# A top-1 attention kernel on one core: half-width screening while the keys load, and a rearranged tail

## Chip, cores, metric

One core of a Trainium2 chip (trn2). The metric is device time in microseconds (us) of one execution, taken from the chip. Engines are called as in the profile: PE (TensorE), PEld (its weight loads), ACT (ScalarE), DVE (VectorE), POOL (GpSimd), SP (SyncE). "Fold" below means the VectorE instruction that writes `W` for one tile of 128 query rows; there are 128 tiles (4 batches of 32), so the starts of the folds are 128 clock marks spread over the run, and nearly every reading below uses them.

## The reference

```python
def setup_inputs():
    B, Sq, Sk, D = 4, 4096, 4096, 128      # q, k, v: randn, float32, fixed seed

def reference(q, k, v):
    logits = np.matmul(q, k.transpose(0, 2, 1))
    best = np.argmax(logits, axis=-1)
    b_idx = np.arange(q.shape[0])[:, None]
    return v[b_idx, best, :].astype(np.float32)
```

For each query row: the key with the largest dot product, and that key's row of `v`.

## The kernel before

The kernel screens groups of four keys in fp16 (the product of a query tile with sums and differences of keys, absolute values, a maximum of 8 per row), then gathers the candidate group, works out its exact dots on VectorE, and gathers the row of `v`. Rows whose best two groups are too near ("flagged") are computed again in fp32 at the end of each half. The parts that the change touches, with cuts:

```python
LATE = 5
...
    def put_first(b, h):                      # first key of each group, negated, for the differences
        ...
        nc.vector.tensor_scalar(out=kd[:, h, :, 0, :], in0=src[:, :, 0, :], scalar1=-1.0, scalar2=None, op0=OP.mult)
...
    def dpart(t, x):                          # differences: product and absolute value
        if t >= T:
            return
        ps = pp.tile([P, 1024], FP32, tag="u", name=f"pd_{t}_{x}")
        mm(ps, t, 1 + 2 * x, True)
        A = ep.tile([P, 1024], FP16, tag=f"A{x}", name=f"A_{t}_{x}")
        nc.scalar.activation(out=A, in_=ps, func=AF.Abs)
        A_t[t, x] = A

    def spart(t, x):                          # sums, plus A; x == 0 leaves PSUM through ScalarE as E
        ...
    def fold(t):                              # x == 1 is folded with E into W on VectorE
        E, ps = E_t.pop(t)
        nc.vector.scalar_tensor_tensor(out=W_t[t % NW].bitcast(I16)[:, 1::2], in0=ps, scalar=QSCALE, in1=E,
                                       op0=OP.mult, op1=OP.max)

    def top(t):
        nc.vector.max(out=TOP[:, t, :], in_=W_t[t % NW].bitcast(FP32))
...
    def dots(c, x, m):                        # exact dots of m tiles at once: prod, p, p, D
        ...
    def flags_last(t0, t1, ready, fill, late):   # flagged rows of the second half, at the very end
        ...
        OH = fp.tile([P, SLOTS, P], FP16, tag="OHe", name="OH_e")
        for z in range(SLOTS):
            nc.vector.tensor_scalar(out=OH[:, z], in0=iota_h, scalar1=posn[:, z:z + 1], scalar2=None, op0=OP.is_equal)
        ...                                   # TensorE adds up fq_e from OH
        fill()
        ...                                   # gb_e, rs_e, row_e read fq_e
        late(LATE)                            # so many waiting gathers of v rows go ahead of FK
        get(FK[:, 0, :], k_flat, gb[:, 0:1], B * Sk)
        get(FQ, q_flat, row, P * T)
        for r in (1, 2):
            get(FK[:, r, :], k_flat, gb[:, r:r + 1], B * Sk)
        yield
        ...                                   # dots of FK with FQ, index xw_fe
        get(FV, v_flat, win, B * Sk)
        nc.gpsimd.indirect_dma_start(out=out_flat, out_offset=IOA(ap=rowk, axis=0), in_=FV, in_offset=None, ...)
...
    put_k(0, 0)                               # head: second half of the first batch's keys
    for u in (1, 3, 0, 2):
        trn_half(u, 1, (0, 1))
    trn_half(1, 1, (2, 3), by_act)
    trn_half(3, 1, (2, 3), by_dve)
    trn_half(0, 1, (2, 3), by_dve)
    trn_half(2, 1, (2, 3), by_dve)
    dpart(0, 0)
    dpart(0, 1)
...
            m = 4 if t1 <= 108 else 2         # tiles per dots
...
    screen(T)                                 # tail
    top(T - 2)
    gathers(T - 2)
    flush()
    fold(T - 1)
    ...
    end = flags_last(T // 2, T, last_picks, lambda: dots_whole(0), late_now)
    next(end)
    dots_whole(1)
    pick_whole()
```

Of the kernel before, what the change touches and what calls it, by code (L numbers as in the profile page):

```python
# [7 lines left out]
FP32 = mybir.dt.float32  # L8
FP16 = mybir.dt.float16
# [6 lines left out]
OP = mybir.AluOpType  # L16
AF = mybir.ActivationFunctionType
# [4 lines left out]
TAU = 8.0  # L22
NEAR = 0.5
SLOTS = 6
LATE = 5
NKG = 6


# [1 line left out]
def kernel(ctx, tc, q, k, v, out):  # L30
    nc = tc.nc
    B, Sq, D = q.shape
    Sk = k.shape[1]
    P = 128
    NQT = Sq // P
    T = B * NQT
# [10 lines left out]
    pp = ctx.enter_context(tc.tile_pool(name="ps", bufs=4, space=bass.MemoryType.PSUM))  # L47
    ep = ctx.enter_context(tc.tile_pool(name="ev", bufs=3))
    rp = ctx.enter_context(tc.tile_pool(name="ref", bufs=2))
    sp = ctx.enter_context(tc.tile_pool(name="sml", bufs=4))  # L50
    fp = ctx.enter_context(tc.tile_pool(name="flag", bufs=1))
# [6 lines left out]
    kT = [bp.tile([P, Sk], FP16, name=f"kT{i}", tag=f"kT{i}") for i in range(2)]  # L58
    qT = [bp.tile([P, Sq], FP16, name=f"qT{i}", tag=f"qT{i}") for i in range(2)]
    natk = [bp.tile([P, 2, 16, P], FP16, name=f"natk{i}", tag=f"natk{i}") for i in range(2)]  # L60
    kd = bp.tile([P, 2, 4, 3, P], FP16, name="kd", tag="kd")
# [9 lines left out]
    def put_k(b, h):  # L71
        if b >= B:
            return
        src = natk[b % 2][:, h].rearrange("p (g f) d -> p g f d", f=4)
        nc.vector.tensor_tensor(out=kd[:, h], in0=src[:, :, 1:4, :], in1=src[:, :, 0:1, :].to_broadcast([P, 4, 3, P]),
                                op=OP.subtract)
        kb16 = k16[b].rearrange("(h p n) d -> p h (n d)", p=P, n=16)
        nc.sync.dma_start(out=kb16[:, h], in_=kd[:, h].rearrange("p g f d -> p (g f d)"))

    def put_first(b, h):  # L80
        if b >= B:
            return
        src = natk[b % 2][:, h].rearrange("p (g f) d -> p g f d", f=4)
        nc.vector.tensor_scalar(out=kd[:, h, :, 0, :], in0=src[:, :, 0, :], scalar1=-1.0, scalar2=None, op0=OP.mult)
        kb16 = k16[b].rearrange("(r x) d -> r (x d)", x=4).rearrange("(h p g) (f d) -> p h g f d", h=2, p=P, f=3)
        for f in range(3):
            nc.sync.dma_start(out=kb16[:, h, :, f, :], in_=kd[:, h, :, 0, :])
# [22 lines left out]
    for i in range(2):  # L110
        ps = pp.tile([P, 1024], FP32, tag="u", name=f"warm_{i}")
# [33 lines left out]
    iota_h = cp.tile([P, P], FP16, tag="iota_h")  # L145
# [5 lines left out]
    for h in range(2):  # L151
# [3 lines left out]
                            op0=OP.mult, op1=OP.add)  # L155
# [20 lines left out]
    def trn_half(u, h, ms, put=None):  # L176
        x = 2 * (u // 2)
        if ms[0] == 0:
            tk_t[u] = pp.tile([P, 512], FP32, tag="u", name=f"tk_{u}_{h}")
        ps = tk_t[u]  # L180
        for m in ms:
            o = ps[:, m * P:(m + 1) * P]
            nc.tensor.matmul(out=o, lhsT=natk[0][:, h, 4 * m + x, :], rhs=identh, start=True, stop=False)
            nc.tensor.matmul(out=o, lhsT=natk[0][:, h, 4 * m + x + 1, :],
                             rhs=identn if u % 2 else identh, start=False, stop=True)
        if put is not None:
            put(kT[0][:, u * 1024 + h * 512:u * 1024 + h * 512 + 512], ps)
# [31 lines left out]
    A_t = {}  # L219
    st = {}  # L220

    def mm(ps, t, u, stop):
        b, qt = t // NQT, t % NQT
        for n in range(2):
            nc.tensor.matmul(out=ps[:, n * 512:(n + 1) * 512], lhsT=qT[b % 2][:, qt * P:(qt + 1) * P],  # L225
                             rhs=kT[b % 2][:, u * 1024 + n * 512:u * 1024 + (n + 1) * 512], start=True, stop=stop)

    def dpart(t, x):
        if t >= T:
            return  # L230
        ps = pp.tile([P, 1024], FP32, tag="u", name=f"pd_{t}_{x}")
        mm(ps, t, 1 + 2 * x, True)
# [3 lines that stand above are left out]
# [16 lines left out]
    def screen(t):  # L252
        dpart(t, 0)
        spart(t - 1, 0)
        dpart(t, 1)
        spart(t - 1, 1)
# [6 lines left out]
    def top(t):  # L263
        nc.vector.max(out=TOP[:, t, :], in_=W_t[t % NW].bitcast(FP32))  # L264
# [201 lines left out]
    def flags_last(t0, t1, ready, fill, late):  # L466
# [16 lines left out]
        ps = pp.tile([P, 1024], FP32, tag="u", name="fp_e")  # L483
        nc.tensor.matmul(out=ps[:, 0:1], lhsT=tri, rhs=n2[:, 0:1], start=True, stop=True)  # L484
        for r in range(1, 4):
# [5 lines left out]
                                op0=OP.is_ge, op1=OP.mult)  # L491
        posn = fp.tile([P, SLOTS], FP32, tag="posn", name="posn_e")
# [2 lines left out]
                                       scalar=-2.0 * Sk, in1=e8[:, 1:4, 0:SLOTS].rearrange("p r s -> p s r"),  # L495
                                       op0=OP.mult, op1=OP.add)
        OH = fp.tile([P, SLOTS, P], FP16, tag="OHe", name="OH_e")
        for z in range(SLOTS):
            nc.vector.tensor_scalar(out=OH[:, z], in0=iota_h, scalar1=posn[:, z:z + 1], scalar2=None, op0=OP.is_equal)
        ps2 = pp.tile([P, 1024], FP32, tag="u", name="fq_e")  # L500
        for s in range(SLOTS):
# [12 lines left out]

        late(LATE)
        get(FK[:, 0, :], k_flat, gb[:, 0:1], B * Sk)
# [49 lines left out]
    def dots_whole(i):  # L566
        for f in range(4):
            pr = fp.tile([P, P], FP32, tag="xp", name=f"xp_w_{i}_{f}", bufs=2)
            nc.vector.tensor_tensor_reduce(out=pr, in0=X_t[i][:, f * P:(f + 1) * P], in1=q32[:, i, :], scale=1.0, scalar=0.0,
                                           op0=OP.mult, op1=OP.add, accum_out=XD[:, i, f:f + 1])  # L570
# [94 lines left out]
    ALL = range(4)  # L665
# [2 lines left out]
    trn_half(0, 0, ALL, by_act)  # L668
    trn_q(0, 4, by_dve)
    trn_half(2, 0, ALL, by_act)  # L670
    put_k(0, 0)
    for u in (1, 3, 0, 2):
        trn_half(u, 1, (0, 1))
    trn_half(1, 1, (2, 3), by_act)
    trn_half(3, 1, (2, 3), by_dve)
    trn_half(0, 1, (2, 3), by_dve)
    trn_half(2, 1, (2, 3), by_dve)
    dpart(0, 0)
    dpart(0, 1)
    nc.vector.tensor_copy(out=iota_h, in_=iota_r)  # L680
    nc.vector.tensor_copy(out=rec2[:, :, 1], in_=iota_p.to_broadcast([P, SLOTS]))
    cuts = list(range(0, 96 + 1, 8)) + list(range(96 + 4, T - 3, 4)) + [T - 2, T]
    chunks = list(zip(cuts[:-1], cuts[1:]))
# [45 lines left out]
    def take_late(n):  # L729
        while n > 0 and late_q:  # L730
            g = late_q.pop(0)
            n -= g not in stores
            g()
        while late_q and late_q[0] in stores:
            wait_q.append((clock[0] + 2, late_q.pop(0)))
# [3 lines left out]
    def put_out(now):  # L739
        while wait_q and wait_q[0][0] <= now:  # L740
            wait_q.pop(0)[1]()

    def issue(it):
        n = 0
        clock[0] = it
        put_out(it)
        behind = len([g for g in near_q if g not in marks]) > (2 if it >= TAIL else 4)
        while near_q and (n < 1 + behind or near_q[0] in marks or it >= T - 1):
            g = near_q.pop(0)
            n += g not in marks  # L750
            g()
        if fast and it >= rest[0]:
            fast.pop(0)()
            rest[0] = it + 2
            n += 1
        if it < 16:
            take_late(2 if n == 0 and len(late_q) > 4 else 1)
            return
        b, qt = it // NQT, it % NQT
        busy = 0.7 if qt % 2 == 0 and (10 <= qt < 18 and b + 1 < B or 18 <= qt < 26 and b + 2 < B) else 0.0  # L760
        if qt in (13, 17) and b + 1 < B:
            busy += 1.0
        rate = 2.45 if it < 72 else 2.65 if it < 80 else 2.45 if it < 96 else 2.6 if it < 104 else 2.45 if it < 112 else 2.6
        room[0] = min(room[0] + rate - busy, 3.0) - n
        for i in range(2):
            if room[0] >= 1 and late_q and it < T - 1:
                take_late(1)
                room[0] -= 1
# [3 lines left out]
    def gathers(t):  # L772
        if t >= T - 2:
            gather_whole(t)
        for c, (t0, t1) in enumerate(chunks):
            m = 4 if t1 <= 108 else 2
            if t0 <= t < t1 and t < T - 2 and (t - t0) % m == m - 1:
                gather(c, t - m + 1, m)
            if t == t0 and t < T - 2:
                start(pick(c, t0, t1), "pick", c)  # L780
        if t % 8 == 7:
            put_rec(t - 7, t + 1)
        if t == SEGS[1] - 1:
            last = [c for c, x in enumerate(chunks) if x[1] == t + 1][0]
            start(flag_segment(0, t + 1, lambda: ("cnt", last) in done, lambda: ("out", last) in done), "flags")
# [3 lines left out]
    for b in range(1, B):  # L789
        x = b * NQT  # L790
        units += [(x - 1, x - NQT + (6 + 3 * i // 2 if b == 1 else 1 + 2 * i), unit_k, b, i) for i in range(16)]
    for it in range(T):
        b, qt = it // NQT, it % NQT
# [7 lines left out]
        if open_units:  # L801
            u = min(open_units)
# [35 lines left out]
    def late_now(n):  # L838
        take_late(n)
        put_out(1 << 20)  # L840

    def drain(group):
        for s in group:
            while True:
                try:
                    y = next(s["g"])
                except StopIteration:
                    live.remove(s)
                    break
                if y[0] == "until":  # L850
                    assert y[1]()

    def left(kind):
        return [s for s in live if s["kind"] == kind]

    screen(T)
    top(T - 2)
    gathers(T - 2)
    flush()
# [8 lines left out]
        drain(left("dots"))  # L868
        drain(left("pick"))

    end = flags_last(T // 2, T, last_picks, lambda: dots_whole(0), late_now)
    next(end)
    dots_whole(1)
    pick_whole()
    for _ in end:
# [32 lines left out]
```

## Time and profile before

| | before |
|---|---|
| median of the timed runs beside the kernel after | 440.71 us (440.14 to 441.29, 4 runs) |
| the profiled execution | 439.86 us, span 437.9 us, granted clock 0.964 |
| first fold; fold of tile 2; fold of tile 126 | 16.46; 21.96; 402.10 us |
| first candidate gather of tiles 122/123 on GpSimd | 399.17 us |
| first FK gather; FV gather; last scatter | 419.12; 429.59; 433.66 us |

A line of a timeline reads: start, duration, engine, line of the kernel, operation, output <- input, shapes, number of instructions merged into the line, and in brackets the idle time of that engine just before it and what ended it. A line of the groups by line has busy time and the mean of one instruction in ns. In the tail, kg, vr and xk are gathers of candidate groups, of values and of whole key rows; FK, FQ and FV are those of keys, queries and values for the flagged rows. The row list is the index `row_e` that the FQ gather reads; it is the last of the indices to come. A transfer lands when the profile shows its data as arrived.

### The profile page before, as it was taken

The numbers are of one execution on the slowest core, as the hardware profiler recorded it, in microseconds if no ns is written. First come the engines' busy times: TensorE is split into PE (matmuls) and PEld (weight loads), VectorE is DVE, ScalarE is ACT, GpSimd is POOL, SyncE is SP. The second block draws the span as 40 slices with busy tenths as digits, with TensorE's granted clock in tenths as the row PEclk, the third lists the DMA queues.
The fourth block names the chain that finished last, engine by engine and source line by source line (L and its number), as shares of the span: only waits on it lengthen the run. The fifth ranks groups of instructions, "written<-read, shape, count | busy, mean of one in ns | idle before, by whom it ended". The sixth has DMA issues, their size and how long they took to land.

```text
span 437.9 us, 6167 instructions
## 1 busy us (share of the span) xinstructions
PE 378.8 (87%) x1830; PEld 168.2 (38%) x1830; DVE 407.8 (93%) x734; ACT 375.5 (86%) x437; POOL 304.9 (70%) x335
## 2 busy tenths in 40 slices
PE   8999999999999999999999889989889888896010
PEld 4444444444444444444444334434333333332010
DVE  2688999999999999999999999999999999999971
ACT  2899999999999999999999789999998988896000
POOL 8513466677757886777777776777777777777773
PEclk9999999999999999999999999999999999999555
DMA  7943999463325999763326985362322332233341
GB/s 124 198 107 67 152 151 149 97 120 86 107 66 130 167 168 188 125 123 103 89 82 150 166 154 115 91 144 81 113 81 82 89 90 84 87 101 99 106 131 55
DMA packets 52868, 50.54 MB, mean 115 GB/s; under 512 B 34136, under 2 KB 40890, under 8 KB 52832
## 3 DMA queue, kind: packets, MB, share of 16 engines
q0 software_dynamic: 19072, 33.87, 38.5%
q1 hardware_dynamic: 33760, 16.26, 14.9%
q8 instruction: 14, 0.23, 0.2%
q14 instruction: 22, 0.18, 0.1%
HBM read 40.05 MB, written 14.55 MB: 125 GB/s over the span
## 4 chain that ended last, share of the span: by engine, by line
ACT 41%; issue 19%; DVE 16%; PE 14%; DMA 6%; POOL 3%; POOLq 0%; ACTq 0%; DVEq 0%; SPq 0%
ACT A L234 34%; ACT E L247 7%; DVE TOP L264 6%; PE psn L225 5%; PE psn L244 4%; DVE W L260 4%; PE pd L225 4%; DMA natk<-in_k_dram 2%; DMA FK<-in_k_dram,gb_e 2%; DMA out_dram<-vr 1%; DVE prod L300 1%; POOL vr L342 1%; POOL kg L282 1%; DVE p L305 1%; DVE D L310 1%
## 5 line engine op out<-in xcount | busy, mean ns | idle before, releaser
L234 ACT ACTIVATE A<-pd 128x1024 f16<-128x1024 f32 x256 | 260.2, 1045 | 13.7 <-PE pd L225 13.4
L282 POOL DMA_INDIRECT kg<-k,cand x126 | 125.5, 996 | 80.1 <-DVE cand L276 49.3
L260 DVE SCALAR_TENSOR_TENSOR W<-psn,E 128x1024 int16<-128x1024 f32 x128 | 166.2, 1298 | 7.2 <-ACT E L247 5.2
L225 PE MATMUL psn<-kT,qT 128*128 128x512 f16 x512 | 151.9, 378 | 13.8 <-ACT A L234 6.0
L225 PE MATMUL pd<-kT,qT 128*128 128x512 f16 x512 | 151.9, 378 | 8.9 <-ACT A L234 8.6
L225 PEld LDWEIGHTS <-qT 128*128 128x128 f16 x1024 | 97.9, 97 | 154.0 <-issue 64.0
L264 DVE MAX8 TOP<-W 128x8 f32<-128x1024 f32 x128 | 155.9, 1218 | 0.0
L342 POOL DMA_INDIRECT vr<-in_v_dram,win x126 | 125.2, 994 | 40.4 <-issue 33.5
L244 PE MATMUL psn<-A,identh 128*128 128x512 f16 x512 | 152.0, 378 | 0.0
L247 ACT ACTIVATE E<-psn 128x1024 int16<-128x1024 f32 x128 | 132.4, 1034 | 3.3 <-PE psn L244 3.0
L244 PEld LDWEIGHTS <-identh 128*128 128x128 f16 x512 | 49.6, 97 | 60.8
L300 DVE TENSOR_TENSOR prod<-kg,natq 128x768 f16<-128x768 f16 x63 | 34.4, 546 | 0.0
L205 ACT ACTIVATE kT<-uk 128x256 f16<-128x256 f32 x48 | 20.5, 427 | 1.5 <-PE uk L202 1.5
L305 DVE TENSOR_TENSOR p<-prod 128x768 f16<-128x768 f16 (+1 forms) x36 | 17.9, 497 | 0.1
L310 DVE TENSOR_REDUCE D<-p 128x12 f32<-128x384 f16 (+1 forms) x36 | 17.5, 486 | 0.1
L201 PE MATMUL uk<-identh,natk 128*128 128x128 f16 x96 | 15.8, 218 | 0.0
L484 PE MATMUL fp_e<-n_e,tri 128*128 128x1 f32 x2 | 0.6, 348 | 13.7 <-DVE n_e L482 13.7
L202 PEld LDWEIGHTS <-natk 128*128 128x128 f16 x96 | 9.3, 97 | 7.1 <-issue 4.7
L66 POOL DMA_DIRECT2D natk<-in_k_dram x19 | 11.3, 600 | 0.8 <-POOLq L892 0.8
L308 DVE TENSOR_TENSOR p<-p 128x384 f16<-128x384 f16 (+1 forms) x36 | 11.6, 322 | 0.3
L201 PEld LDWEIGHTS <-natk 128*128 128x128 f16 x96 | 9.4, 98 | 5.6
L69 POOL DMA_DIRECT2D natq<-in_q_dram x15 | 9.1, 612 | 0.0
(152 smaller groups left out, 140.2 us busy)
## 6 DMA issues: line engine op xcount, KB each, us to landing
out_dram<-vr SPq DMA_DIRECT2D x31, 256.0 KB, 2.2
natq<-in_q_dram POOLq DMA_DIRECT2D x12, 256.0 KB, 6.8
natk<-in_k_dram POOLq DMA_DIRECT2D x10, 256.0 KB, 4.6
k<-kd SPq DMA_DIRECT2D x18, 128.0 KB, 3.4
k<-natk POOLq DMA_DIRECT2D x6, 384.0 KB, 6.6
kg<-k,cand POOLq DMA_INDIRECT x126, 2.7
vr<-in_v_dram,win POOLq DMA_INDIRECT x126, 2.6
natk<-in_k_dram POOLq DMA_DIRECT2D x8, 128.0 KB, 5.2
```

The costliest lines, as they stand in the source:

```text
L201: nc.tensor.matmul(out=o, lhsT=natk[b % 2][:, h, 4 * m + x, :], rhs=identh, start=True, stop=False)
L225: nc.tensor.matmul(out=ps[:, n * 512:(n + 1) * 512], lhsT=qT[b % 2][:, qt * P:(qt + 1) * P], rhs=kT[b % 2][:, u * 1024 + n * 512:u * 1024 ...
L234: nc.scalar.activation(out=A, in_=ps, func=AF.Abs)
L244: nc.tensor.matmul(out=ps[:, n * 512:(n + 1) * 512], lhsT=identh, rhs=A[:, n * 512:(n + 1) * 512], start=False, stop=True)
L247: nc.scalar.activation(out=E, in_=ps, func=AF.Relu, scale=QSCALE)
L260: nc.vector.scalar_tensor_tensor(out=W_t[t % NW].bitcast(I16)[:, 1::2], in0=ps, scalar=QSCALE, in1=E, op0=OP.mult, op1=OP.max)
L264: nc.vector.max(out=TOP[:, t, :], in_=W_t[t % NW].bitcast(FP32))
L282: near_q.append(lambda j=j: nc.gpsimd.indirect_dma_start(out=kg[:, j].rearrange("p f d -> p (f d)"), out_offset=None, in_=k16[t0 // NQT], ...
L300: nc.vector.tensor_tensor(out=prod[:, i:i + h], in0=kg[:, i:i + h], in1=natq[b % 2][:, x + i - b * NQT:x + i + h - b * NQT, :].unsqueeze(2 ...
L305: nc.vector.tensor_tensor(out=p1, in0=prod[:, :, :, 0:64], in1=prod[:, :, :, 64:128], op=OP.add)
L310: nc.vector.tensor_reduce(out=d[:, x - c0:x - c0 + m, 1:4], in_=p2, axis=AX_X, op=OP.add)
L342: late_q.append(lambda j=j: nc.gpsimd.indirect_dma_start(out=vr[:, j, :], out_offset=None, in_=v_flat, in_offset=IOA(ap=win[:, i + j:i + j ...
```

## The change

Four parts. (1) Head: the first halves of three absolute values (tiles 0 and 1) are made from the first half of the keys while the second half is still on its way; only the second halves remain after it has landed. (2) The negated first keys of the last batch move from VectorE to ScalarE. (3) The dots of tiles 108 to 115 are done for four tiles at once instead of two. (4) Tail: dots and pick of tiles 120 to 123 ahead of the last two maxima, one gather of values less ahead of FK, two of the six one-hots of the last flagged rows on ScalarE, and the whole-row dots behind the reading of TensorE's sum.

```diff
-LATE = 5
+LATE = 4
@@ put_first @@
+        if b == B - 1:
+            nc.scalar.activation(out=kd[:, h, :, 0, :], in_=src[:, :, 0, :], func=AF.Copy, scale=-1.0)
+        else:
+            nc.vector.tensor_scalar(out=kd[:, h, :, 0, :], ...)
@@ new @@
+    def dhalf(t, x, n):
+        ps = pp.tile([P, 512], FP32, tag="u", name=f"ph_{t}_{x}_{n}")
+        nc.tensor.matmul(out=ps, lhsT=qT[0][:, t * P:(t + 1) * P],
+                         rhs=kT[0][:, (1 + 2 * x) * 1024 + n * 512:(1 + 2 * x) * 1024 + (n + 1) * 512], start=True, stop=True)
+        if n == 0:
+            A_t[t, x] = ep.tile([P, 1024], FP16, tag=f"A{x}", name=f"A_{t}_{x}")
+        nc.scalar.activation(out=A_t[t, x][:, n * 512:(n + 1) * 512], in_=ps, func=AF.Abs)
@@ dpart @@
-        if t >= T:
+        if t >= T or (t, x) in A_t:
@@ flags_last @@
-        for z in range(SLOTS):
+        far = fp.tile([P, 2, P], FP16, tag="far", name="far_e")
+        for z in (SLOTS - 2, SLOTS - 1):
+            w = far[:, z - SLOTS + 2]
+            nc.scalar.activation(out=w, in_=iota_h, func=AF.Abs, scale=-1.0, bias=posn[:, z:z + 1])
+            nc.scalar.activation(out=OH[:, z], in_=w, func=AF.Relu, scale=-1.0, bias=1.0)
+        for z in range(SLOTS - 2):
             nc.vector.tensor_scalar(out=OH[:, z], ...)
@@ head @@
+    for t, x in ((0, 0), (0, 1), (1, 0)):
+        dhalf(t, x, 0)
     put_k(0, 0)
-    for u in (1, 3, 0, 2):
-        trn_half(u, 1, (0, 1))
+    trn_half(1, 1, (0, 1))
+    trn_half(3, 1, (0, 1))
     ...
-    trn_half(0, 1, (2, 3), by_dve)
-    trn_half(2, 1, (2, 3), by_dve)
-    dpart(0, 0)
-    dpart(0, 1)
+    trn_half(0, 1, ALL, by_dve)
+    trn_half(2, 1, ALL, by_dve)
+    for t, x in ((0, 0), (0, 1), (1, 0)):
+        dhalf(t, x, 1)
@@ gathers @@
-            m = 4 if t1 <= 108 else 2
+            m = 4 if t1 <= 116 else 2
@@ tail @@
+        if it == T - 1:
+            take_late(1)
...
     screen(T)
+    drain([x for x in left("dots") if x["c"] == len(chunks) - 3])
+    drain(left("pick")[:1])
+    late_now(1)
     top(T - 2)
...
-    end = flags_last(T // 2, T, last_picks, lambda: dots_whole(0), late_now)
+    end = flags_last(T // 2, T, last_picks, lambda: None, late_now)
     next(end)
+    dots_whole(0)
     dots_whole(1)
```

More of the change, by code (lines that the diff above doesn't have):

```diff
@@ L83, in put_first @@
         src = natk[b % 2][:, h].rearrange("p (g f) d -> p g f d", f=4)
-        nc.vector.tensor_scalar(out=kd[:, h, :, 0, :], in0=src[:, :, 0, :], scalar1=-1.0, scalar2=None, op0=OP.mult)
+        if b == B - 1:
+            nc.scalar.activation(out=kd[:, h, :, 0, :], in_=src[:, :, 0, :], func=AF.Copy, scale=-1.0)
+        else:
+            nc.vector.tensor_scalar(out=kd[:, h, :, 0, :], in0=src[:, :, 0, :], scalar1=-1.0, scalar2=None, op0=OP.mult)
         kb16 = k16[b].rearrange("(r x) d -> r (x d)", x=4).rearrange("(h p g) (f d) -> p h g f d", h=2, p=P, f=3)
```

## The prediction

> **What bounds the kernel now.** I read the page's busy shares first, then the table by stretches, then the timelines of the two ends. The page says that three engines are nearly full:
>
> ```profile
> PE 378.8 (87%) x1830; PEld 168.2 (38%) x1830; DVE 407.8 (93%) x734; ACT 375.5 (86%) x437; POOL 304.9 (70%) x335
> ```
>
> The table by stretches (PE, PEld, DVE, ACT, POOL busy of 20 us, with instruction counts) says where:
>
> ```profile
> 0.00:20.00 20.00, 17.97 (x116) 9.22 (x117) 8.21 (x18) 11.01 (x14) 15.32 (x38) 1.00 0.91 163
> 20.00:40.00 20.00, 19.21 (x98) 8.71 (x96) 16.62 (x16) 20.00 (x25) 5.25 (x6) 1.00 0.55 100
> ...
> 120.00:140.00 20.00, 19.69 (x98) 8.86 (x97) 20.00 (x29) 20.00 (x25) 13.52 (x14) 1.00 0.40 102
> ...
> 380.00:400.00 20.00, 17.92 (x77) 7.25 (x75) 19.66 (x39) 17.82 (x20) 15.43 (x16) 1.00 0.31 91
> 400.00:420.00 20.00, 3.60 (x18) 1.84 (x16) 18.86 (x73) 1.75 (x2) 13.86 (x15) 0.65 0.36 101
> ```
>
> Up to about 50 us ScalarE (ACT) sets the pace and VectorE (DVE) has gaps; from 50 to 220 us both are full; from 220 us on DVE alone is full while ACT loses 1 to 4 us per stretch. GpSimd (POOL) looks 77% busy at 380 to 400 us, but each of its gathers is followed by a gap of 0.30 us that no reordering takes away: 16 gathers are 15.43 + 16 x 0.30 = 20.2 us, so POOL is full too. What can be won lies at the head, in DVE work after 220 us, and in the tail.
>
> The head, in the timeline of ACT and DVE:
>
> ```profile
> 9.40 0.60 ACT L190 ACTIVATE kT<-tk 128x512 f16<-128x512 f32 x1 [0.35 <-PE tk L184]
> ...
> 11.38 0.60 ACT L190 ACTIVATE kT<-tk 128x512 f16<-128x512 f32 x1 [1.38 <-PE tk L184]
> ...
> 12.66 2.85 ACT L234 ACTIVATE A<-pd 128x1024 f16<-128x1024 f32 x3 [0.68 <-PE pd L225]
> ...
> 15.39 1.04 ACT L247 ACTIVATE E<-psn 128x1024 int16<-128x1024 f32 x1
> ...
> 16.46 1.31 DVE L260 SCALAR_TENSOR_TENSOR W<-psn,E 128x1024 int16<-128x1024 f32 x1 [2.60 <-ACT E L247]
> ```
>
> ACT idles 1.38 us until the second half of the keys has landed (10.9 us in the chain of waits), then makes three absolute values in a row, and only then can the first E and the first fold W come.
>
> The tail, in the timeline of POOL (gathers: kg candidate groups, vr values, xk whole rows of the last two tiles, FK/FQ/FV for flagged rows):
>
> ```profile
> 399.17 0.96 POOL L282 DMA_INDIRECT kg<-k,cand  x1 [0.30 <-DVE cand L276]
> ...
> 405.23 0.96 POOL L282 DMA_INDIRECT kg<-k,cand  x1 [1.15 <-DVE cand L276]
> ...
> 413.80 1.01 POOL L342 DMA_INDIRECT vr<-in_v_dram,win  x1 [1.23 <-DVE near L323]
> ...
> 419.12 1.05 POOL L512 DMA_INDIRECT FK<-in_k_dram,gb_e  x1 [0.41 <-DVE row_e L509]
> ...
> 429.59 1.00 POOL L512 DMA_INDIRECT FV<-in_v_dram,xw_fe  x1 [0.30 <-issue]
> 433.66 1.02 POOL L541 DMA_INDIRECT out_dram<-FV,rowk_e  x1 [3.08 <-DMA out_dram<-vr]
> ```
>
> The first FK gather waits for DVE's row list, which ends at 419.11. Then eight gathers run back to back (FK, FQ, FK, FK, four vr) until FV at 429.59. The last scatter waits for the last store of values, as the chain of waits shows:
>
> ```profile
> 428.29 2.52 DMA vr<-in_v_dram,win_w
> 430.81 0.02 SPq L346
> ...
> 430.89 1.78 DMA out_dram<-vr
> ```
>
> It lands at 432.67; the scatter starts 0.99 us later, and the span ends 4.24 us after that.
>
> [...] in the groups by shape:
>
> ```profile
> L305 DVE TENSOR_TENSOR p<-prod 128x768 f16<-128x768 f16 x27 | 14.7, 546 | 0.1
> ...
> L305 DVE TENSOR_TENSOR p<-prod 128x384 f16<-128x384 f16 x9 | 3.1, 348 | 0.1
> ```
>
> [...] Here a vr gather takes 2.6 us from issue to landing at the median and FV 2.4[...].
>
> **The change part by part.**
>
> (1) Head. Three half-width products and absolute values go into ACT's gap. [...] TensorE meanwhile does all transposes of the second half before the second half-products (24 after landing at 0.055 us each, to 12.3). [...] The first E can start once TensorE has added up its sums. These reuse the PSUM buffer that DVE empties last at 13.50 (today's three casts, 11.61 + 1.89), so 13.55 + about 1.05 = 14.6, against 15.39. ACT is the bound here, so up to 0.8 us is carried on; I take 0.7.
>
> (2) The negated first keys of the last batch leave DVE for ACT: two instructions, 0.19 us apart from their successors at 242 us, in a stretch where DVE is full and ACT busy only 16.21 of 20: 0.4 us off DVE.
>
> (3) Four-tile dots for tiles 108 to 115. Per four tiles, one of each replaces two: (2 x 348 - 546) + (2 x 258 - 344) + (2 x 343 - 533) for the folding sums, and 2 x 219 - 167 for the candidate step = 0.75 us of busy time; four fewer instructions that each overlap a neighbour by about 0.07, so 0.45. Two chunks: 0.9 us.
>
> (4) Tail up to FK. The dots and pick of tiles 120 to 123 (1.54 + 0.97 us) only move ahead of the last two TOPs; DVE has no gap there, so its sum is unchanged. Out of the path go two one-hots (0.36) and the four whole-row dots (0.84) that stood between TensorE's sum (done at 418.17) and its reading (418.69). [...]
>
> POOL allows less. In the order of instructions, 14 gathers lie today between the first kg gather of tiles 122/123 (399.17) and FK, with two waits of together 1.8 us over the unavoidable gaps. After the change there are 16, as one vr more is ahead of FK and one comes later past that kg gather. That gather is ready 2.0 us earlier (parts 1 to 3): 397.1; POOL just keeps up until then (30 gathers from tile 108's on x 1.28 = 38.4 us, against 38.6 of DVE work). 6 x 1.26 + 10 x 1.30 = 20.6 puts FK at 417.7: 1.4 us earlier, with POOL the one that ends last.
>
> (5) After FK. Seven gathers now lie before FV instead of eight, so POOL is free at FK + 9.1. But FV's index needs the third FK: issued at FK + 3.96, landing 4.15 later (423.08 to 427.23), index 1.82 after that (429.05): FK + 9.95. Today it is FK + 10.47. The last store lands at FK + 6.56 + 2.52 + 0.08 + 1.78 = FK + 10.9; FV lands at FK + 12.35 and is now what the scatter waits for: with 0.99, FK + 13.35, today FK + 14.54. Won: 1.2 us.
>
> Sum: 1.4 + 1.2 = 2.6 us, 441.2 - 2.6 = 438.6 us, 0.6% less.
>
> **The rivals.**
>
> (a) DVE, not POOL, ends last before FK. For it: today FK is released by the row list, POOL having waited 0.11 us. Against it: two more gathers in the same stretch. It would give 0.8 us more, 437.8.
>
> (b) The head's gain is not carried on. For it: the ACT copy of kT goes behind the half values, the PSUM buffers go round in fours, and TensorE has 24 transposes left instead of 16. Against it: the first E today plainly waits for ACT. Then 439.3.
>
> (c) The tail turns into waits for gathers: the kg gathers of tiles 122/123 are spread (one vr in between, three behind), so the second lands at about the moment its dots now want it; DVE stalls, or the xk and FK gathers queue behind vr. Up to 1 us: 439.6; with (b), 440.4.
>
> (d) The ACT one-hots come last of all. As POOL has the last word, nothing; under (a), it is why only 0.25 is won.
>
> **Range and chances.** All rivals lie within 437.8 and 440.4, and runs of the kernel before spread from 440.21 to 441.29. So 436.6 to 440.6 should hold it 8 times in 10. A gain of 2% is 8.8 us, more than three times everything counted here: faster 0.01, same 0.98, slower 0.01.
>
> **What would show it.** First E at 14.6 us, first W near 15.7; tile 0's gain still there at 200 us; the candidate step of tiles 120/121 about 2.0 us earlier than 391.92; gathers back to back from 397 us to FK with FK's releaser on POOL itself; FV released by its index and the scatter by FV, not by a store. I am wrong if the E of tile 0 does not move, if POOL waits for DVE's row list again, or if DVE shows gaps before the dots of tiles 122/123.

Cut in (1) are the times of the half values and of the copy behind them, which the sum for the first E (14.6 us) does not contain, and in (4) those of ScalarE's one-hots, with the two results that came of them: 0.25 us won, and FK at 416.9 by VectorE alone. (a) has 0.8 us (417.7 less 416.9) and (d) 0.25. The traces show: on ScalarE 0.60 us for a copy of 512 elements a row, 1.045 us at the mean for an absolute value of 1024, and 2.85 us for three of these in a row where three times the mean is 3.13. The two lines of the groups by shape in the text give the 546 and 348 ns of (3).

## The result

The changed kernel is correct and took 438.55 us at the median (438.37 to 438.78, 4 runs), the kernel before 440.71 us in the same rounds. The ratio is 0.9951 with a 95% interval of 0.9933 to 0.9969: within 2%. Times the 440.71 us, the interval means 1.4 to 3.0 us saved.

The page of the changed kernel: VectorE lost 1.2 us of busy time (407.8 before), ScalarE gained 2.7 us.

```profile
PE 377.1 (86%) x1830; PEld 167.7 (38%) x1830; DVE 406.6 (93%) x722; ACT 378.2 (87%) x446; POOL 304.3 (70%) x335
```

The most useful view is none of these but a subtraction: the start of each tile's fold after the change minus that before, from the two timelines of VectorE.

| fold of tile | before | after | difference |
|---|---|---|---|
| 0 | 16.46 | 15.64 | -0.82 |
| 2 | 21.96 | 20.82 | -1.14 |
| 72 | 227.68 | 226.53 | -1.15 |
| 80 | 254.91 | 253.35 | -1.56 |
| 108 | 342.73 | 341.16 | -1.57 |
| 116 | 369.58 | 366.20 | -3.38 |
| 123 | 392.00 | 390.18 | -1.82 |
| 126 | 402.10 | 400.28 | -1.82 |
| 127 | 406.20 | 406.95 | +0.75 |

So the head gives 1.14 us, the negated keys between tiles 72 and 80 another 0.41, the four-tile dots between 108 and 123 only 0.25 (tile 116 is ahead by more because its neighbours' dots now come later, bunched). Each part acts in a stretch of its own, and the negated keys come in two steps of 0.21 and 0.19 us, at tiles 73 and 77; no undisturbed run takes one of these parts out alone. The fold of tile 127 comes later since 2.5 us of dots and pick now stand ahead of it; that is a move, not a cost.

The head, in ScalarE's timeline after the change: the first three half values fill what was a gap of 1.38 us, and the copy of the second half of `kT` still starts at once.

```profile
9.50 1.57 ACT L237 ACTIVATE A<-ph 128x512 f16<-128x512 f32 x3
11.22 0.60 ACT L193 ACTIVATE kT<-tk 128x512 f16<-128x512 f32 x1 [0.15 <-PE tk L187]
12.56 1.57 ACT L237 ACTIVATE A<-ph 128x512 f16<-128x512 f32 x3 [0.74 <-PE ph L233]
14.27 1.02 ACT L258 ACTIVATE E<-psn 128x1024 int16<-128x1024 f32 x1
```

The negated keys, in VectorE's timeline of the kernel before and in ScalarE's of the kernel after (the second of the two instructions in each): 0.27 us on VectorE become 0.63 us on ScalarE, which had room.

```profile
242.14 0.27 DVE L84 TENSOR_SCALAR kd<-natk 128x512 f16<-128x512 f16 x1
```

```profile
237.99 0.63 ACT L85 ACTIVATE kd<-natk 128x512 f16<-128x512 f16 x1
```

The four-tile dots, in the table by stretches from the fold of tile 108 to the fold of tile 126 (columns: stretch, length, then PE, PEld, DVE, ACT and POOL busy with instruction counts, clock, DMA share, GB/s), before:

```profile
342.73:402.10 59.37, 52.17 (x219) 21.01 (x217) 58.62 (x110) 51.63 (x55) 44.84 (x47) 1.00 0.31 93
```

and after:

```profile
341.16:400.28 59.12, 51.98 (x221) 21.11 (x218) 57.98 (x102) 51.92 (x55) 43.59 (x45) 1.00 0.32 89
```

VectorE's busy time fell by 0.64 us, but the stretch by 0.25: its gaps grew from 59.37 - 58.62 = 0.75 to 59.12 - 57.98 = 1.14 us. The second undisturbed profile with four-tile dots (one-hots back on VectorE, below) has 57.96 us busy of 59.11, so the same. Two waits that the timeline of before does not have make up this difference. In the first, two tiles without any dots follow each other, VectorE gets through fold and maximum in 2.6 us and then waits 0.25 us for ScalarE; in the second the two-tile dots behind the last bunch wait 0.16 us for a gather to land. The one-hot run has the same two waits, of 0.19 and 0.21 us.

```profile
364.75 1.21 DVE L275 MAX8 TOP<-W 128x8 f32<-128x1024 f32 x1
366.20 1.31 DVE L271 SCALAR_TENSOR_TENSOR W<-psn,E 128x1024 int16<-128x1024 f32 x1 [0.25 <-ACT A L245]
...
384.54 0.56 DVE L311 TENSOR_TENSOR prod<-kg,natq 128x768 f16<-128x768 f16 x1 [0.16 <-DMA kg<-k,cand]
```

The tail, in GpSimd's timeline after the change. From the first candidate gather of tiles 122/123 (397.23) to the last value gather (426.44) all gathers run back to back, each followed by its gap of 0.30 us.

```profile
397.23 0.96 POOL L293 DMA_INDIRECT kg<-k,cand  x1 [0.47 <-DVE cand L287]
...
418.51 1.01 POOL L528 DMA_INDIRECT FK<-in_k_dram,gb_e  x1 [0.30 <-DVE XD L585]
...
426.44 1.02 POOL L353 DMA_INDIRECT vr<-in_v_dram,win_w  x1 [0.30 <-issue]
428.30 1.00 POOL L528 DMA_INDIRECT FV<-in_v_dram,xw_fe  x1 [0.84 <-DVE xw_fe L623]
432.35 1.02 POOL L557 DMA_INDIRECT out_dram<-FV,rowk_e  x1 [3.05 <-DMA out_dram<-vr]
```

FV is released by its index, as predicted. The scatter, though, is still released by the store of values and not by FV. In the chain of waits the last value gather and its store take

```profile
426.44 2.75 DMA vr<-in_v_dram,win_w
429.27 2.09 DMA out_dram<-vr
```

which lands at 431.36, 0.99 us ahead of the scatter. And VectorE waits 0.91 us for TensorE's sum over the one-hots, since the two that ScalarE makes come last (they end at 416.64, VectorE's four at 416.01):

```profile
416.92 0.16 DVE L521 TENSOR_SCALAR gb_e<-fq_e 128x3 uint32<-128x3 f32 x1 [0.91 <-PE fq_e L518]
...
417.18 0.15 DVE L525 TENSOR_SCALAR row_e<-rs_e 128x1 uint32<-128x1 f32 x1
```

Counted from 399.17 (before) and 397.23 (after), the last value gather starts 29.12 and 29.21 us later: 21 gathers and 1.8 us of waits before, 22 gathers and no wait after. The rearranged tail starts its last value gather no sooner relative to the work ahead of it. Had the old tail moved as it was by the 1.82 us of the fold of tile 126, FK would have started at 417.30 and the last value gather at 426.47 (an estimate from the timeline of before): with the new tail FK is 1.2 us later than that, with two more gathers ahead of it, and the last value gather stands at the same place. In this pair the scatter gained 1.31 us and the span 1.4 us, less than the 2.16 us of the timed medians, because before's profiled execution was a quick one.

### The profile page after: what moved, and what is told of

It is laid out like the page before. It is cut to its first block, busy times and chain, and to the rows that moved or that the text cites. A ratio compares the mean times of both kernels' runs of the same rounds, so it can differ in the third digit from the quotient of the medians.

```text
span 436.5 us, 6165 instructions
## 1 busy us (share of the span) xinstructions
PE 377.1 (86%) x1830; PEld 167.7 (38%) x1830; DVE 406.6 (93%) x722; ACT 378.2 (87%) x446; POOL 304.3 (70%) x335
## 4 chain that ended last, share of the span: by engine, by line
ACT 37%; issue 23%; DVE 16%; PE 9%; POOL 8%; DMA 6%; POOLq 0%; ACTq 0%; DVEq 0%; SPq 0%
ACT A L245 32%; DVE TOP L275 6%; ACT E L258 5%; DVE W L271 5%; POOL vr L353 4%; PE psn L228 3%; POOL kg L293 3%; PE pd L228 3%; PE psn L255 3%; DMA vr<-in_v_dram,win 2%; DMA natk<-in_k_dram 2%; DVE prod L311 1%; DVE p L316 1%; DMA vr<-in_v_dram,win_w 1%; DMA kg<-k,cand 1%
## 5 line engine op out<-in xcount | busy, mean ns | idle before, releaser
L245 ACT ACTIVATE A<-pd 128x1024 f16<-128x1024 f32 x253 | 257.0, 1043 | 10.8 <-PE pd L228 10.3
```

## The experiments

Twelve runs were made, of nine kernels. Theory A is the account just read from the profiles (head about 1.1, keys 0.4, four-tile dots 0.25, tail nothing because GpSimd's train of gathers sets the end). Theory B is the prediction with its sizes (0.7, 0.4, 0.9, tail 0.6 or more).

**A warning on eleven of the twelve.** All but one ran in a disturbed state in which every kernel, the one before included, took 507 to 553 us instead of 441 (mean granted clock 0.89 to 0.93 instead of 0.96). The expectations call it throttled; what causes it is not known, as shown below. In the table by stretches of one of these runs (the change without its tail, first run) a disturbed stretch lies beside an untouched one:

```profile
140.00:160.00 20.00, 14.57 (x59) 5.73 (x58) 11.79 (x21) 12.82 (x15) 9.43 (x11) 0.83 0.48 94
160.00:180.00 20.00, 19.59 (x99) 8.72 (x98) 20.00 (x28) 19.94 (x26) 14.71 (x16) 1.00 1.00 163
```

In the first, VectorE is busy for 11.79 of 20 us although its instructions last as long as ever (a fold 1.30 us, a maximum 1.22 us). The timeline of the same stretch shows TensorE with nothing to wait for and yet idle:

```profile
144.23 0.59 PE L228 MATMUL psn<-kT,qT 128*128 128x512 f16 x2 [2.32 <-issue]
```

ScalarE and VectorE then wait for it (ScalarE 2.11 us up to 143.16, VectorE 2.88 us up to 150.55). In this stretch the lower clock is not what stops TensorE. Cut finer, the 0.83 is a mean of 1.00 and 0.50, and the idle time comes first, at full clock:

```profile
142.00:144.00 2.00, 0.00 (x0) 0.00 (x0) 0.00 (x0) 0.84 (x1) 1.55 (x2) 1.00 0.69 148
147.00:153.00 6.00, 4.62 (x12) 1.57 (x11) 3.12 (x6) 3.88 (x4) 0.98 (x1) 0.50 0.57 114
```

Why TensorE stops stays open. So in these runs the bottleneck is another, the times of one kernel spread by 1 to 5%, and neither their times nor their ratios say anything on a change of 0.5%. Two things in them can be used: the first 85 us or so, where the clock is 1.00 and the difference between two runs' folds stays the same to 0.04 us from tile to tile, and what releases a gather in the tail. Only the run with the one-hots back on VectorE (on a chip of its own) was undisturbed.

### Head alone, tail alone, four-tile dots alone, all but the tail (one chip, one call, disturbed)

Head alone is the kernel before with the new function `dhalf`, the test in `dpart` and the head sequence of the diff above, nothing else.

> The kernel before with the head alone (half-width products and absolute values while the second key half loads). Theory A, from the fold starts of the two profiles: folds W from tile 3 on are 1.0 to 1.15 us earlier than before and stay so to tile 124; the end moves by the same, about -1.1 us (ratio 0.9975). Theory B, my prediction: 0.7 us at most. Theory C: the head's gain is lost by 200 us, and the folds there stand where they stood.

Measured: 522.50 us against 529.39, ratio 0.9955 (0.9824 to 1.0086), unclear.

Tail alone is the kernel before with

```diff
-LATE = 5
+LATE = 4
+        for z in (SLOTS - 2, SLOTS - 1):      # two one-hots on ScalarE
...
+        if it == T - 1:
+            take_late(1)
...
+    drain([x for x in left("dots") if x["c"] == len(chunks) - 3])
+    drain(left("pick")[:1])
+    late_now(1)
...
-    end = flags_last(T // 2, T, last_picks, lambda: dots_whole(0), late_now)
+    end = flags_last(T // 2, T, last_picks, lambda: None, late_now)
+    dots_whole(0)
```

> The kernel before with the tail alone (dots of tiles 120 to 123 sooner, two one-hots on ScalarE, whole-row dots after the row list, one value gather moved). Theory A: from the last candidate gathers on GpSimd issues gathers back to back to the last value gather, and the tail part only reorders them, so the end moves by no more than 0.5 us either way (0.0, ratio 0.999 to 1.001). Theory B, my prediction: FK a little later or at the same place and the end 0.6 to 1.2 us earlier, ratio 0.9975. Folds W of tiles 0 to 126 do not move in either.

Measured: 523.99 us, ratio 1.0012 (0.9916 to 1.0109), unclear.

All but the tail is the changed kernel with the tail's lines undone (the diff above, backwards).

> The changed kernel with its tail part undone: head, negated keys on ScalarE and four-tile dots stay. Theory A: the end is 1.5 to 2.1 us earlier than before, as early as the changed kernel's or a few tenths earlier (ratio 0.9955 +- 0.0015). Theory B, my prediction: the tail is worth 0.6 us, so only 1.9 us of its 2.6 are left, and the changed kernel stays ahead of this one by 0.6. The fold of tile 124 stands 1.8 us earlier than before in both.

Measured: 527.65 us. Four-tile dots alone is the kernel before with

```diff
-            m = 4 if t1 <= 108 else 2
+            m = 4 if t1 <= 116 else 2
```

> The kernel before with four-tile dots to tile 116 alone. Theory A: VectorE's removed work comes back as waits for ScalarE and TensorE in tiles without dots (gaps before W of tiles 116 and 120), so the fold of tile 124 is only 0.25 us earlier (0.1 to 0.4) and the end the same within noise. Theory B, my prediction: 0.9 us earlier at tile 124 and at the end.

Measured: 526.43 us. All four were correct.

What the four tell is in their first 98 us. With the head, in the timelines of the weight loads and of VectorE (first transposition of the second half of the keys; fold of tile 2):

```profile
10.99 0.10 PEld L183 LDWEIGHTS <-natk 128*128 128x128 f16 x1 [0.63 <-DMA natk<-in_k_dram]
```

```profile
21.02 1.32 DVE L268 SCALAR_TENSOR_TENSOR W<-psn,E 128x1024 int16<-128x1024 f32 x1 [0.19 <-ACT E L255]
```

and with the head of before, in the run with the tail alone:

```profile
11.10 0.10 PEld L183 LDWEIGHTS <-natk 128*128 128x128 f16 x1 [0.42 <-DMA natk<-in_k_dram]
```

```profile
22.11 1.31 DVE L260 SCALAR_TENSOR_TENSOR W<-psn,E 128x1024 int16<-128x1024 f32 x1 [0.34 <-ACT E L247]
```

From the landing of the second half, which these loads mark, to the fold of tile 2 it is 10.03 us with the new head and 11.01 with the old. All 14 profiles say the same:

| | first transposition of the second half | to the fold of tile 2 |
|---|---|---|
| old head: before, tail alone, four-tile alone | 10.95, 11.10, 11.07 | 11.01, 11.01, 11.02 |
| new head: after | 10.79 | 10.03 |
| new head: the 10 other runs | 10.90 to 11.19 | 10.03 or 10.04 |

So the head is worth 0.98 us, and the load's landing scatters by 0.4 us from run to run and is passed on in full. The 1.14 us of the first pair contain 0.16 us of such luck. Until the disturbance sets in (after 98 us in these runs) the difference stays as it is, and in the undisturbed pair until the negated keys: the head's gain is carried on. Of Theory A the head stands, a little smaller than the first pair showed; of rival (b) in the prediction, that it is not carried on, nothing. The other three parts can't be read from these runs.

### All but the tail again, and two gathers fewer (same disturbed state)

The first is the same kernel.

> The same kernel as in the run without the tail part, once more, because the chip of that run was throttled (all kernels 18% slow). Theory A: 1.5 to 2.1 us earlier than before (ratio 0.9955 +- 0.0015), level with the changed kernel or a few tenths ahead of it. Theory B, my prediction: the tail is worth 0.6 us or more, so this version lies 0.6 us behind the changed kernel.

Measured: 524.68 us against 529.93, ratio 0.9871 (0.9783 to 0.9958), unclear; disturbed again.

The second is the changed kernel without the value gathers of tiles 118 and 119, whose rows stay unwritten: wrong (the test that marks the group as done, further down, is widened to match).

```diff
     def put_values(c, i, n, win, dst):
         ...
         m = min(4, n - i)
+        if chunks[c] == (116, 120):
+            m, dst = 2, dst[:, 0:2]
```

> The changed kernel with two value gathers left out (tiles 118 and 119 stay unwritten: wrong on purpose). Theory A, a full train of gathers on GpSimd sets the end: the first FK gather moves up by about 1.1 us until VectorE's row list holds it, the last value gather by 2.5 us, and the end by 1.3 to 1.8 us beyond the changed kernel (ratio to before 0.992). Theory B, VectorE's chain sets the end: FK stays within 0.3 us of its place and the end does not move beyond the changed kernel (ratio 0.995).

Measured: 524.74 us, ratio 0.9915 (0.9831 to 0.9998), unclear. The numbers expected of it did not come: the scatter came 24.28 us after the fold of tile 127 (25.40 in the changed kernel undisturbed), but screening is slowed so much there that GpSimd has caught up before the tail, with or without the two gathers. For that very reason one thing can be read. In its timeline the row list and the first FK gather are

```profile
503.11 0.15 DVE L527 TENSOR_SCALAR row_e<-rs_e 128x1 uint32<-128x1 f32 x1
```

```profile
503.27 1.10 POOL L530 DMA_INDIRECT FK<-in_k_dram,gb_e  x1 [1.06 <-issue]
```

GpSimd has been idle, and FK starts 0.16 us after the row list. It is 0.16 or 0.17 us in all four disturbed runs that have the whole of the new tail (tail alone, two gathers fewer twice, and the one below with four-tile dots only to 108). Undisturbed, where GpSimd runs back to back, it starts 418.51 - 417.18 = 1.33 us after it. Whichever of the two comes last sets FK, and undisturbed that is GpSimd.

### One-hots back on VectorE (undisturbed)

```diff
-        for z in (SLOTS - 2, SLOTS - 1):
-            w = far[:, z - SLOTS + 2]
-            nc.scalar.activation(out=w, in_=iota_h, func=AF.Abs, scale=-1.0, bias=posn[:, z:z + 1])
-            nc.scalar.activation(out=OH[:, z], in_=w, func=AF.Relu, scale=-1.0, bias=1.0)
-        for z in range(SLOTS - 2):
+        for z in range(SLOTS):
             nc.vector.tensor_scalar(out=OH[:, z], ...)
```

> The changed kernel with all six one-hots of the last flagged rows on VectorE again, everything else as changed. This is also the look that shows whether the chip is still throttled (earlier calls ran on a chip whose granted TensorE clock fell to 0.74 to 0.93 after 100 us). Theory A (account from the profiles): in the changed kernel the two one-hots on ScalarE end about 0.9 us after the four on VectorE (reading of the sum waited 0.91 us), and six on VectorE take only 2 x 0.18 us more; so the row list ends 0.3 to 0.6 us earlier relative to the fold of tile 127 than in the changed kernel (10.23 us), at 9.6 to 9.9. If GpSimd's train of gathers sets the first FK gather, FK and the end do not move (FK at fold of tile 127 + 11.56, end + 29.55, each within 0.2). Theory B (my prediction, that the ScalarE one-hots win 0.25): the row list ends 0.25 later, at 10.5, and nothing else moves either. If the row list set the end (rival a), the end would move with it.

Measured: correct, 439.38 us in one run against 441.61 for one run of the kernel before on the same chip (clock 0.96): 2.23 us less. VectorE's timeline:

```profile
417.10 0.16 DVE L516 TENSOR_SCALAR gb_e<-fq_e 128x3 uint32<-128x3 f32 x1 [0.28 <-PE fq_e L513]
...
417.36 0.15 DVE L520 TENSOR_SCALAR row_e<-rs_e 128x1 uint32<-128x1 f32 x1
```

The fold of tile 127 starts at 407.43 here and at 406.95 in the changed kernel. So the row list comes 9.93 us after it instead of 10.23: the one-hots on ScalarE cost 0.30 us instead of winning 0.25. But FK does not care:

```profile
419.00 1.00 POOL L523 DMA_INDIRECT FK<-in_k_dram,gb_e  x1 [0.30 <-DVE XD L580]
```

is 11.57 us after that fold, against 11.56. This is the prediction's rival (d) under GpSimd's lead, and Theory A, whose 9.6 to 9.9 for the row list is missed by 0.03 and whose FK is met. A row list that comes 0.3 us earlier moves nothing, so rival (a), VectorE having the last word before FK, is out.

The end, expected at fold + 29.55 within 0.2, came at + 30.17 and thus was missed. The chain of waits shows why:

```profile
426.82 3.68 DMA vr<-in_v_dram,win_w
430.59 1.82 DMA out_dram<-vr
```

The last value gather was issued at nearly the same moment relative to the fold (19.39 against 19.49) and took 0.93 us longer to land. Over the ten profiles in which this gather lies in the chain of waits its landing took 2.35 to 3.68 us. As all else in this run repeats the changed kernel's shifts (0.41 between tiles 72 and 80, 0.26 between 108 and 123), an undisturbed run seems to differ from the next by the landing of the second half of the keys (0.4 us) and of the last gather (up to 1.3 us), and by little else.

### Three more looks at single parts, and two attempts at a better version (disturbed)

All but the tail for the third time, four-tile dots only to tile 108 in the changed kernel (`m = 4 if t1 <= 108 else 2`), and two gathers fewer again:

> The changed kernel without its tail (dots of tiles 120 to 123 not moved ahead, five late value gathers ahead of FK, six one-hots on VectorE, whole-row dots before the reading of the sum), third time, now that the granted clock is back at 0.96. Theory A (account from the two profiles: head -1.15, negated keys -0.4, four-tile dots -0.25, tail about 0 because GpSimd's train of gathers from the first candidate gather of tiles 122/123 sets the end): 438.6 to 439.0 us, so 0 to 0.4 us more than the changed kernel; the fold of tile 126 is 1.8 us earlier than before, and from the fold of tile 127 to the end 31.7 us as before. Theory B (my prediction, tail worth 0.6 at least): 439.2 us or more. Per-tile fold shifts against before: -1.15 from tile 2, -1.55 from tile 80, -1.8 at 123.

> The changed kernel with four-tile dots only to tile 108 again (108 to 116 in twos). Theory A (four-tile dots save what the sums say in VectorE's busy time but VectorE then runs ahead of ScalarE and TensorE in the tiles without dots and waits for them): the folds of tiles 116 to 126 come 0.2 to 0.4 us later than in the changed kernel, although VectorE's busy time from tile 108 to 118 is 0.4 to 0.8 us more; VectorE's gaps there are smaller. Time 438.6 to 439.0. Theory B (my prediction, 0.45 per four tiles): folds 0.9 later, time 439.4.

> The changed kernel with the value gathers of tiles 118 and 119 left out (these rows stay unwritten: wrong on purpose), again, now at the normal clock. Theory A (GpSimd's train of gathers sets the first FK gather and the last store): FK 1.1 us earlier (then the row list releases it), the last value gather 2.5 earlier, FV at the first FK + 9.8 released by its index, the scatter released by FV's landing instead of the store, the end 1.6 to 1.8 us earlier relative to the fold of tile 127; time 436.8 to 437.1. Rival (VectorE's chain or a landing sets the end and GpSimd only follows): the end moves by less than 0.5, time 438.2 or more.

Measured, on another chip against 529.84 us for the kernel before: 520.99, 523.81 and 528.49 us (the last wrong). The disturbance set in between the folds of tiles 28 and 33, at 98 to 115 us. No expectation on the folds after tile 28 or on the end could be tested; their heads are in the table above.

The first attempt takes the one-hots the other way round: those of the first half's flagged rows, made at 246 to 249 us where VectorE is full and ScalarE waits up to 0.7 us per tile, go to ScalarE, and those of the last rows back to VectorE.

```diff
+        yield "wait", 1
+        near1 = fp.tile([P, 2, P], FP16, tag="near1", name=f"near1_{t0}")
         for z in range(SLOTS):
-            nc.vector.tensor_scalar(out=OH[:, z], in0=iota_h, scalar1=posn[:, z:z + 1], scalar2=None, op0=OP.is_equal)
-            if z % 2:
-                yield "dve", 0.17
+            nc.scalar.activation(out=near1[:, z % 2], in_=iota_h, func=AF.Abs, scale=-1.0, bias=posn[:, z:z + 1])
+            nc.scalar.activation(out=OH[:, z], in_=near1[:, z % 2], func=AF.Relu, scale=-1.0, bias=1.0)
+            yield "wait", 2
```

> An attempt at a better version: the changed kernel with the one-hots the other way round: the six of the first half's flagged rows (at 246 to 249 us, where VectorE is full and ScalarE waits 0.5 to 0.7 us per tile) go to ScalarE, one per two tiles, and the two of the last rows go back to VectorE. Theory A (VectorE time before the tail counts in full until the end, as the negated keys showed; in the tail the one-hots are off the path): the six cost VectorE 6 x about 0.17 = 1.0 us, so the folds from tile 84 on come 0.8 to 1.0 us earlier than in the changed kernel, and the end as well: 437.6 to 437.8 us. Rival (ScalarE's 12 added instructions of 0.3 to 0.4 us delay E or A, since ScalarE's slack is only 0.2 us per tile from 285 us on): 0 to 0.5 earlier, 438.1 to 438.6.

Measured: correct, 515.86 us in the same rounds. It has the lowest median of that call, but with a spread of 509.75 to 526.45 that shows nothing. The order in which the program was built also told of a fault: spreading the one-hots over twelve tiles delays the flagged rows' gathers, and two more value gathers are then left over for the tail.

The second attempt mends that (one one-hot per tile, and 0.05 more in the rate at which value gathers are let out from tile 88 on) and leaves the new tail out, so that it would have told the tail's worth too:

```diff
-            yield "wait", 2
+            yield "wait", 1
...
+        rate += 0.05 if it >= 88 else 0.0
         room[0] = min(room[0] + rate - busy, 3.0) - n
```

> Head, negated keys and four-tile dots of the change; the tail as in the kernel before; and, new, the six one-hots of the first half's flagged rows (246 to 249 us in the changed kernel) on ScalarE, one per tile. An attempt at a better version that also settles the tail, if the granted clock is back at 0.96. Read from the start of each tile's fold against the kernel before. Theory A: the head gives 0.75 to 1.15 from tile 2 on; between tiles 72 and 84 another 0.4 (negated keys); from tile 84 to 112 another 0.8 to 1.0 (six one-hots of 0.17 us of VectorE's time each, where VectorE is the only full engine); the tail is worth nothing, so from the fold of tile 127 to the end it is 31.7 us as before (within 0.6, the spread of the last gather's landing), and the 21 gathers from the first candidate gather of tiles 122/123 to the last value gather take 29.1 us within 0.3. Time 437.6 to 438.4. Theory B (my prediction): the tail is worth 0.6 at least, so the whole gains no more than the changed kernel although the one-hots give 0.9: 438.6 to 439.0, and the 21 gathers take 29.7 or more. Rival for the one-hots: ScalarE has only 0.5 us of slack per tile there and each costs it 0.6, so the folds gain under 0.4 between tiles 84 and 112.

Measured: correct, 544.12 us at the median against 538.87, ratio 1.0161 (1.0036 to 1.0287), unclear, in the worst disturbance of all (it began before 99 us). Neither theory can be judged by it. Whether this version beats the changed kernel stays open.

## Why the prediction was right, and where it was right by luck

The total was right: 438.6 us predicted, 438.55 measured. That it is right to 0.05 us is luck: it was 441.2, the median of the three runs of before then known, less 2.6. A fourth run put that median at 440.71, and 2.16 us were saved, so a base 0.5 us too high and a gain 0.44 us too large cancel. The terms of the gain were not all of the right size.

| step | predicted | shown |
|---|---|---|
| 1 head | 0.7 | 0.98 (plus 0.16 of luck with a landing in the first pair) |
| 2 negated keys | 0.4 | 0.41, twice |
| 3 four-tile dots | 0.9 | 0.25 and 0.26 |
| 4 tail up to FK | FK 1.4 earlier, GpSimd last | FK 0.61 earlier, GpSimd last |
| 5 after FK | 1.2 | 0.70 in the pair |

**Step 1** was right in its mechanism. First E at 14.27 (14.6 predicted), first fold at 15.64 (15.7), gain kept to the end. One term was too pessimistic: the copy of the second half of the keys was to be pushed back by the first three half values (an estimate of the author's, cut above). These ran from 9.50 to 11.07, and it was not pushed back at all (0.43 us after the first transposition in both kernels). The first fold itself is now released by TensorE's sum and not by E (VectorE idle for 2.09 us, ended by PE), so it gains only 0.82 us in the pair; 1.14 is reached at tile 2, which waits for E again (0.18 us). And 0.7 was a discount on 0.8 that nothing asked for.

**Step 2** was right; 0.2 us of VectorE per instruction counted in full where VectorE alone is full.

**Step 3** is the term that was mis-sized most. "So 0.45" for four tiles was durations less overlap, 0.9 in all (from 362 to 370 us of the timeline of before, most neighbours on VectorE overlap by 0.03 to 0.11 us). Eight instructions fewer between the folds of tiles 108 and 126 took only 0.64 us of busy time away, and 0.39 of that came back as gaps. One wait of 0.25 us is for ScalarE: work in bunches of four leaves tiles with no dots at all, and there VectorE outruns it. Another of 0.16 us is for a gather, in the dots that follow the last bunch. The prediction's own table had the sign of the first: ScalarE was idle only 1 to 4 us per 20 us there. "VectorE is full on average" was read as "VectorE is the bound in every tile".

**Step 4.** GpSimd had the last word, as predicted and as the one-hot run shows, and its train started as predicted (397.23, predicted 397.1). The sum of the train, 20.6 us for 16 gathers, measured 21.28: five of them took 1.05 to 1.37 us where 0.96 to 1.00 was put in. Why these are slower stays open. The 0.25 us that ScalarE's one-hots were to win were a loss of 0.30, off the path. Rival (c), a tail that waits for gathers, did not come: the dots of tiles 122/123 start at 410.20 without a gap on VectorE.

**Step 5** holds an error of arithmetic. "The last store lands at FK + 6.56 + 2.52 + 0.08 + 1.78" starts from the first of the two gathers for the last two tiles; the store needs the second, 1.30 us later. With it the store lands at FK + 12.2, level with FV's landing at FK + 12.35, and the two were a toss-up. Measured, the store landed at FK + 12.85 and released the scatter. Of the 0.6 us beyond 12.25, 0.23 are the gather's longer landing and 0.31 its longer store (2.75 and 2.09 us, against 2.52 and 1.78). In the eight disturbed runs where FV released it, the scatter came 2.82 to 3.33 us after the start of FV, which from 428.30 would have been 0.7 to 1.2 us sooner than 432.35.

**The sum.** Steps 1 to 3 without luck give 0.98 + 0.41 + 0.25 = 1.64 us. The timed runs say 2.16, with an interval from 1.4 to 3.0. So the first three parts carry most of the result, and for the tail there remains something between a small loss and 1.3 us. The profiles point to little: from the fold of tile 126 to the end it is 35.8 us before, 36.22 in the changed kernel and 36.85 with the one-hots back on VectorE, while the last value gather and its store took 4.38, 4.92 and 5.59 us. Without these two the new tail is 0.1 or 0.2 us shorter than the old one. That they took longer in both profiles with the new tail may be chance. The tail's net worth is not settled: every run that left it out was disturbed. Corrected step by step, the prediction would have been about 439.6 on its own base (441.2 less 1.64) and 439.1 on the measured one.

## What to carry to other kernels

Subtract the starts of a repeated instruction between two profiles: it places a gain of 0.2 us in a run of 440, where the times of whole runs scatter by 0.5 us and more. Take work off an engine that is full on average only after asking whether its neighbours can feed it faster in the very tiles where the work goes away; if they can't, part of the saving comes back as gaps (here 0.39 of 0.64 us). In a tail that ends with a train of gathers, count the gathers from the one that starts the train: reordering them moved nothing here (29.12 us from the start of the first to that of the last before, 29.21 after); what would count is a train that gets shorter or starts sooner.
